# Wider loads, whole-tile stores and program order in a batched x·yᵀ kernel

## The chip, the cores and the metric

The kernel runs on one core of a Trainium2 chip. The metric is the device time of one execution in microseconds (us). A core has TensorE (PE) for matmuls, VectorE (DVE), ScalarE (ACT) and GpSimd (POOL) for elementwise work, SyncE (SP), which here issues every transfer, and 16 DMA engines that move data between device memory (HBM) and on-chip memory. One transfer is split over all 16 engines, and each of them adds one to the transfer's completion count.

A ratio is the mean time of one kernel's fast runs over that of the other's fast runs of the same rounds, with a 95% interval; it is not quite the ratio of the medians that are quoted.

## The reference

```python
batch, n_heads, seq_t, seq_s, channels = 8, 12, 512, 512, 64
def reference(x, y):                      # x, y: (8, 12, 512, 64) float32
    return np.einsum('bhtc,bhsc->bhts', x, y).astype(np.float32)
```

There are 96 heads, each a 512x64 by 64x512 product. Inputs are 25.2 MB, the output is 100.7 MB, so most of the traffic is stores.

## The kernel before

Eight heads make a group, twelve groups in all. A group's x and y are one load of 1 MB each: 128 partitions, two runs of 16 rows x 64 channels x 4 bytes = 4 KB. GpSimd casts to bf16, TensorE transposes, VectorE and ScalarE copy the transposes out, four 64-row matmuls fill one 128x1024 block of PSUM, and VectorE or ScalarE evicts it. A result tile is two heads, 2 MB, 16 KB in each partition, and goes out in one store, except for the first two and the last two tiles ("edge"), which go in two halves of 8 KB a partition. Loads are kept three groups ahead; six result buffers exist.

```python
    G = 4; Q = P // G; R = T // Q; NG = B * H // (2 * G); K = R // 2; AHEAD = 3
    xv = x...rearrange("(g a p n) -> g p a n", a=2, p=P, n=R * C)          # R * C * 4 = 4 KB
    lpool = ...tile_pool(name="lpool", bufs=AHEAD)
    opool = ...tile_pool(name="opool", bufs=6)
    def load(g):
        ...
        nc.sync.dma_start(ys.rearrange("p a r c -> p a (r c)"), yv[g])
        nc.sync.dma_start(xs.rearrange("p a r c -> p a (r c)"), xv[g])
    ...
    for g in range(NG):
        xT, yT = made.pop(g)
        steps = prepare(g + 1, made) if g + 1 < NG else iter(())   # next group's casts, transposes
        for a in range(2):
            for pair in range(2):
                ot = opool.tile([P, K, S], fp32)
                edge = (g == 0 and a == 0) or (g == NG - 1 and a == 1)
                for k in range(K // 2):
                    ...                                            # next(steps) at blocks 0, 3, 6 of two tiles
                    for two in range(2):
                        for h in range(2):
                            col = (2 * pair + h) * Q
                            nc.tensor.matmul(pm[h * 64:(h + 1) * 64, two, :],
                                xT[a * C:(a + 1) * C, 2 * k + two, col:col + Q]...,
                                yT[a * C:(a + 1) * C, (2 * pair + h) * S:(2 * pair + h + 1) * S], ...)
                    ...                                            # evict pm to ot: ACT or DVE
                    if edge and k % 2 == 1:
                        nc.sync.dma_start(ov[g, 2 * a + pair][:, i:j], otf[:, i:j])
                if not edge:
                    nc.sync.dma_start(ov[g, 2 * a + pair], otf)
```

Of the kernel before, what the change touches and what calls it, by code (L numbers as in the profile page):

```python
# [1 line left out]

# [5 lines left out]


@with_exitstack  # L10
def kernel(
    ctx: ExitStack,
    tc: tile.TileContext,
    x: bass.AP,
    y: bass.AP,
    out: bass.AP,
):





    nc = tc.nc
    B, H, T, C = x.shape
    _, _, S, _ = y.shape
    P = 128
    G = 4
    Q = P // G
    R = T // Q
    NG = B * H // (2 * G)  # L30
    K = R // 2
    AHEAD = 3
    fp32 = mybir.dt.float32
    bf16 = mybir.dt.bfloat16
    COPY = mybir.ActivationFunctionType.Copy
    assert C * 2 == P and S == T and R == 16

    xv = x.rearrange("b h t c -> (b h t c)").rearrange("(g a p n) -> g p a n", a=2, p=P, n=R * C)
    yv = y.rearrange("b h t c -> (b h t c)").rearrange("(g a p n) -> g p a n", a=2, p=P, n=R * C)
    ov = out.rearrange("b h t s -> (b h t s)").rearrange("(g a p n) -> g a p n", a=4, p=P, n=K * S)  # L40

    const = ctx.enter_context(tc.tile_pool(name="const", bufs=1))
    lpool = ctx.enter_context(tc.tile_pool(name="lpool", bufs=AHEAD))
    bpool = ctx.enter_context(tc.tile_pool(name="bpool", bufs=2))
    tpool = ctx.enter_context(tc.tile_pool(name="tpool", bufs=2))
    opool = ctx.enter_context(tc.tile_pool(name="opool", bufs=6))
    ptpool = ctx.enter_context(tc.tile_pool(name="ptpsum", bufs=2, space=bass.MemoryType.PSUM))
    pmpool = ctx.enter_context(tc.tile_pool(name="pmpsum", bufs=3, space=bass.MemoryType.PSUM))

    loaded = {}  # L50

    def load(g):
        xs = lpool.tile([P, 2, R, C], fp32)
        ys = lpool.tile([P, 2, R, C], fp32)
        nc.sync.dma_start(ys.rearrange("p a r c -> p a (r c)"), yv[g])  # L55
        nc.sync.dma_start(xs.rearrange("p a r c -> p a (r c)"), xv[g])  # L56
        loaded[g] = (xs, ys)

    for g in range(AHEAD):
        load(g)  # L60

    ident = const.tile([P, P], bf16)
    make_identity(nc, ident)

    def prepare(g, made):

        xs, ys = loaded.pop(g)
        yb = bpool.tile([P, R, 2, C], bf16)
        xb = bpool.tile([P, R, 2, C], bf16)
        for s, b in ((ys, yb), (xs, xb)):  # L70
            for half in range(2):
                rows = slice(half * K, (half + 1) * K)
                nc.gpsimd.tensor_copy(b[:, rows], s[:, :, rows].rearrange("p a r c -> p r a c"))  # L73
        if g + AHEAD < NG:
            load(g + AHEAD)
        yield
        yT = tpool.tile([P, G * Q, R], bf16)
        xT = tpool.tile([P, K, P, 2], bf16)
        for half in range(2):
            pt = ptpool.tile([P, K, P], bf16)  # L80
            for k in range(K):
                nc.tensor.transpose(  # L82
                    pt[:, k, :], yb[:, half * K + k].rearrange("p a c -> p (a c)"), ident
                )
            dst = yT[:, :, half * K:(half + 1) * K]
            src = pt.rearrange("p k n -> p n k")
            if half == 0:
                nc.vector.tensor_copy(dst, src)  # L88
            else:
                nc.scalar.activation(dst, src, COPY)  # L90
            yield
        for half in range(2):
            pt = ptpool.tile([P, K, P], bf16)
            for k in range(K):
                e, i = divmod(k, K // 2)
                nc.tensor.transpose(  # L96
                    pt[:, k, :], xb[:, e * K + half * K // 2 + i].rearrange("p a c -> p (a c)"), ident
                )
            dst = xT[:, half * K // 2:(half + 1) * K // 2]
            src = pt.rearrange("p (e i) n -> p i n e", e=2)  # L100
            if half == 0:
                nc.vector.tensor_copy(dst, src)  # L102
            else:
                nc.scalar.activation(dst, src, COPY)  # L104
            yield
        made[g] = (xT, yT.rearrange("p n k -> p (n k)"))

    made = {}
    for _ in prepare(0, made):
        pass  # L110
    for g in range(NG):
        xT, yT = made.pop(g)
        steps = prepare(g + 1, made) if g + 1 < NG else iter(())
        for a in range(2):
            for pair in range(2):
                ot = opool.tile([P, K, S], fp32)
                otf = ot.rearrange("p r s -> p (r s)")
                edge = (g == 0 and a == 0) or (g == NG - 1 and a == 1)
                for k in range(K // 2):
                    if (pair * K // 2 + k) in (0, 3, 6):  # L120
                        next(steps, None)
                    pm = pmpool.tile([P, 2, S], fp32)
                    for two in range(2):
                        for h in range(2):
                            col = (2 * pair + h) * Q
                            nc.tensor.matmul(  # L126
                                pm[h * 64:(h + 1) * 64, two, :],
                                xT[a * C:(a + 1) * C, 2 * k + two, col:col + Q].rearrange("c n e -> c (n e)"),
                                yT[a * C:(a + 1) * C, (2 * pair + h) * S:(2 * pair + h + 1) * S],
                                start=True, stop=True,  # L130
                            )
                    if k % 2 == 0:
                        nc.scalar.activation(ot[:, 2 * k:2 * k + 2, :], pm, COPY)  # L133
                    else:
                        nc.vector.tensor_copy(ot[:, 2 * k:2 * k + 2, :], pm)  # L135
                    if edge and k % 2 == 1:
                        i, j = (2 * k - 2) * S, (2 * k + 2) * S
                        nc.sync.dma_start(ov[g, 2 * a + pair][:, i:j], otf[:, i:j])
                if not edge:
                    nc.sync.dma_start(ov[g, 2 * a + pair], otf)  # L140


# [1 line left out]
_INS = ['x', 'y']  # L144
_OUTS = [((8, 12, 512, 512), 'float32')]


# [23 lines left out]
```

## Time and profile before

| what | before | how to read it |
|---|---|---|
| time, median of the first three runs | 306.65 us | the profile is of another, faster execution: 306.08 us, span from first to last instruction 304.3 us |
| bytes on the data queue | 125.83 MB | loads 25.2, stores 100.7 |
| data packets | 6144 of 4 KB, 1024 of 8 KB, 5632 of 16 KB | a packet is one contiguous run of one partition |
| median packet | 159, 309, 611 ns | for 4, 8 and 16 KB |
| busiest compute engine | PE, 69% | but the evictions behind it waited for stores to free result buffers: 81.2 us on ScalarE, 55.4 us on VectorE |
| last store's 16 completions | 296.63 to 303.21 us | the spread of one transfer's completions over the 16 DMA engines |

A transfer counts as landed when the slowest of its 16 engines is done. In the first load of this kernel the 16 completions lie within 0.5 us of each other, in the last store within 6.6 us. I call that spread the **lag**, the first completion the lead engine's, and the average of the 16 the mean engine's. The lines of the page are shown with the prediction.

### The profile page before, as it was taken

How to read it: one execution, taken by the hardware profiler on the slowest of the kernel's cores; microseconds unless marked ns; L12 is line 12 of the kernel's file. 1: busy time of each engine (PE TensorE's matmuls, PEld its weight loads, DVE VectorE, ACT ScalarE, POOL GpSimd, SP SyncE). 2: the span in 40 equal slices, each digit the busy share in tenths (PEclk: the TensorE clock that was granted, in tenths of full speed). 3: DMA queues.
4: the chain of work that ended last, by engine and by line, in shares of the span. 5: the costliest groups of instructions: out<-in, count | busy, mean ns of one | idle time of the engine just before them, and what ended most of it. 6: DMA issues, size and time to landing. Idle time of an engine off the chain costs nothing.

```text
span 304.3 us, 2968 instructions
## 1 busy us (share of the span) xinstructions
PE 208.5 (69%) x1152; PEld 104.6 (34%) x1152; DVE 144.7 (48%) x120; ACT 119.4 (39%) x121; POOL 49.3 (16%) x54
## 2 busy tenths in 40 slices
PE   0899999999959538928946844893897797671000
PEld 0444344555425114513613522541453443330000
DVE  0456666567446435616525733743565664443000
ACT  1454645364445224624515512542364552522000
POOL 3773220400500310230050050031000000000000
PEclk9999999999999855555555655555555555555555
DMA  7999999999999999999999999999999999999992
GB/s 283 411 410 418 436 429 423 419 442 405 445 419 419 430 431 421 420 437 424 426 426 435 414 429 433 413 433 429 433 433 429 431 433 429 428 428 433 423 420 89
DMA packets 14031, 126.03 MB, mean 414 GB/s; under 512 B 1216, under 2 KB 1216, under 8 KB 7360
## 3 DMA queue, kind: packets, MB, share of 16 engines
q1 hardware_dynamic: 14016, 125.83, 98.2%
q8 instruction: 9, 0.15, 0.2%
q14 instruction: 6, 0.05, 0.0%
HBM read 25.17 MB, written 100.66 MB: 413 GB/s over the span
## 4 chain that ended last, share of the span: by engine, by line
DMA 60%; PE 23%; DVE 4%; ACT 2%; issue 1%; POOL 1%; SPq 0%; ACTq 0%
DMA out_dram<-ot 48%; PE pm L126 17%; DMA xs<-in_x_dram 12%; PE pt L82 3%; PE pt L96 3%; DVE ot L135 2%; ACT ot L133 2%; DVE xT L102 1%; POOL xb L73 1%; SPq L55 0%; ACTq L133 0%; SPq L140 0%; ACT xT L104 0%; SPq L56 0%
## 5 line engine op out<-in xcount | busy, mean ns | idle before, releaser
L126 PE MATMUL pm<-yT,xT 64*64 64x512 bf16 x768 | 164.0, 610 | 56.0 <-ACT ot L133 53.9
L135 DVE COPY ot<-pm 128x1024 f32<-128x1024 f32 x96 | 117.2, 1223 | 113.3 <-PE pm L126 57.3
L133 ACT ACTIVATE ot<-pm 128x1024 f32<-128x1024 f32 x96 | 95.1, 1023 | 113.7 <-DMA out_dram<-ot 81.2
L126 PEld LDWEIGHTS <-xT 64*64 64x64 bf16 x768 | 66.1, 150 | 131.2 <-issue 122.7
L73 POOL CAST yb<-ys 128x1024 bf16<-128x1024 f32 x24 | 24.3, 1040 | 140.5 <-DMA ys<-in_y_dram 94.7
L82 PE MATMUL pt<-ident,yb 128*128 128x128 bf16 x192 | 23.7, 307 | 10.7 <-POOL yb L73 6.9
L73 POOL CAST xb<-xs 128x1024 bf16<-128x1024 f32 x24 | 24.3, 1040 | 16.3 <-issue 6.9
L82 PEld LDWEIGHTS <-yb 128*128 128x128 bf16 x192 | 19.9, 143 | 20.3 <-issue 11.5
L96 PE MATMUL pt<-ident,xb 128*128 128x128 bf16 x192 | 24.9, 310 | 1.1 <-POOL xb L73 0.9
L96 PEld LDWEIGHTS <-xb 128*128 128x128 bf16 x192 | 19.1, 141 | 19.3 <-issue 17.8
L104 ACT ACTIVATE xT<-pt 128x1024 bf16<-128x1024 bf16 x12 | 12.3, 1024 | 32.9 <-PE pt L96 29.4
L102 DVE COPY xT<-pt 128x1024 bf16<-128x1024 bf16 x12 | 14.7, 1223 | 10.8 <-PE pt L96 9.4
L88 DVE COPY yT<-pt 128x1024 bf16<-128x1024 bf16 x12 | 14.6, 1216 | 8.9 <-PE pt L82 8.9
L90 ACT ACTIVATE yT<-pt 128x1024 bf16<-128x1024 bf16 x12 | 12.3, 1022 | 9.3 <-PE pt L82 7.7
L90 ACT ACT_TABLE_LOAD x1 | 1.3, 1283 | 0.7 <-PEq L155 0.7
masks.py:199 POOL TENSOR_SCALAR_AFFINE_SELECT ident<-ident 128x128 bf16<-128x128 bf16 x1 | 0.3, 292 | 0.1
masks.py:197 POOL MEMSET ident<- 128x128 bf16 x1 | 0.2, 204 | 0.3 <-POOLq L155 0.3
L155 POOL MEMSET const-float32-0.0<- 128x1 f32 x1 | 0.1, 98 | 0.2 <-issue 0.2
L155 POOL MEMSET const-bfloat16-1.0<- 128x1 bf16 x1 | 0.1, 101 | 0.0
L155 POOL MEMSET const-uint8-127<- 128x1 uint8 x1 | 0.1, 101 | 0.0
L155 POOL MEMSET const-float32-1.0<- 128x1 f32 x1 | 0.1, 98 | 0.0
## 6 DMA issues: line engine op xcount, KB each, us to landing
out_dram<-ot SPq DMA_DIRECT2D x44, 2048.0 KB, 28.3
ys<-in_y_dram SPq DMA_DIRECT2D x12, 1024.0 KB, 20.3
xs<-in_x_dram SPq DMA_DIRECT2D x12, 1024.0 KB, 22.2
out_dram<-ot SPq DMA_DIRECT2D x8, 1024.0 KB, 21.0
```

The source lines that it names most:

```text
L73: nc.gpsimd.tensor_copy(b[:, rows], s[:, :, rows].rearrange("p a r c -> p r a c"))
L82: nc.tensor.transpose(pt[:, k, :], yb[:, half * K + k].rearrange("p a c -> p (a c)"), ident)
L88: nc.vector.tensor_copy(dst, src)
L90: nc.scalar.activation(dst, src, COPY)
L96: nc.tensor.transpose(pt[:, k, :], xb[:, e * K + half * K // 2 + i].rearrange("p a c -> p (a c)"), ident)
L102: nc.vector.tensor_copy(dst, src)
L104: nc.scalar.activation(dst, src, COPY)
L126: nc.tensor.matmul(pm[h * 64:(h + 1) * 64, two, :], xT[a * C:(a + 1) * C, 2 * k + two, col:col + Q].rearrange("c n e -> c (n e)"), yT[a * ...
L133: nc.scalar.activation(ot[:, 2 * k:2 * k + 2, :], pm, COPY)
L135: nc.vector.tensor_copy(ot[:, 2 * k:2 * k + 2, :], pm)
L155: nc = _bacc.Bacc("TRN2", target_bir_lowering=False, num_devices=1)
```

## The change

Its intent is fewer and longer runs: sixteen heads a group (six groups), two 2 MB loads for each with 8 KB runs, two groups ahead (so four load tiles of 2 MB), whole-tile stores everywhere, and every engine's instructions kept in the order in which the program states them, instead of the scheduler's order.

```diff
-    G = 4
+    G = 8                      # R = 32: runs of R * C * 4 = 8 KB
-    K = R // 2
-    AHEAD = 3
+    K = 8
+    E = R // K
+    AHEAD = 2
-    ov = ...rearrange("(g a p n) -> g a p n", a=4, p=P, n=K * S)
+    ov = ...rearrange("(o p n) -> o p n", p=P, n=K * S)
-    bpool = ctx.enter_context(tc.tile_pool(name="bpool", bufs=2))
+    xbpool = ctx.enter_context(tc.tile_pool(name="xbpool", bufs=1))
+    ybpool = ctx.enter_context(tc.tile_pool(name="ybpool", bufs=3))
+        nc.sync.dma_start(xs.rearrange("p a r c -> p a (r c)"), xv[g])
         nc.sync.dma_start(ys.rearrange("p a r c -> p a (r c)"), yv[g])
-        nc.sync.dma_start(xs.rearrange("p a r c -> p a (r c)"), xv[g])
... (prepare: x first in four casts, four transposed blocks; then y in four; the next
...  loads are issued with the last y cast)
-                    if edge and k % 2 == 1:
-                        i, j = (2 * k - 2) * S, (2 * k + 2) * S
-                        nc.sync.dma_start(ov[g, 2 * a + pair][:, i:j], otf[:, i:j])
-                if not edge:
-                    nc.sync.dma_start(ov[g, 2 * a + pair], otf)
+        nc.sync.dma_start(ov[o], ot.rearrange("p r s -> p (r s)"))
+    with tc.manual_schedule():
+        for g in range(AHEAD):
+            load(g)
...
+            for m in range(G):
+                result(g * G + m, steps)
```

More of the change, by code (lines that the diff above doesn't have):

```diff
@@ L35 @@
     COPY = mybir.ActivationFunctionType.Copy
-    assert C * 2 == P and S == T and R == 16
+    assert C * 2 == P and S == T and R == 32 and 2 * Q * E == P
     xv = x.rearrange("b h t c -> (b h t c)").rearrange("(g a p n) -> g p a n", a=2, p=P, n=R * C)
     yv = y.rearrange("b h t c -> (b h t c)").rearrange("(g a p n) -> g p a n", a=2, p=P, n=R * C)
-    ov = out.rearrange("b h t s -> (b h t s)").rearrange("(g a p n) -> g a p n", a=4, p=P, n=K * S)
+    ov = out.rearrange("b h t s -> (b h t s)").rearrange("(o p n) -> o p n", p=P, n=K * S)
     const = ctx.enter_context(tc.tile_pool(name="const", bufs=1))
     lpool = ctx.enter_context(tc.tile_pool(name="lpool", bufs=AHEAD))
-    bpool = ctx.enter_context(tc.tile_pool(name="bpool", bufs=2))
+    xbpool = ctx.enter_context(tc.tile_pool(name="xbpool", bufs=1))
+    ybpool = ctx.enter_context(tc.tile_pool(name="ybpool", bufs=3))
     tpool = ctx.enter_context(tc.tile_pool(name="tpool", bufs=2))
@@ L48 @@
     pmpool = ctx.enter_context(tc.tile_pool(name="pmpsum", bufs=3, space=bass.MemoryType.PSUM))
-    loaded = {}
+    loaded, made = {}, {}
     def load(g):
@@ L54, in load, with copy @@
         ys = lpool.tile([P, 2, R, C], fp32)
+        nc.sync.dma_start(xs.rearrange("p a r c -> p a (r c)"), xv[g])
         nc.sync.dma_start(ys.rearrange("p a r c -> p a (r c)"), yv[g])
-        nc.sync.dma_start(xs.rearrange("p a r c -> p a (r c)"), xv[g])
         loaded[g] = (xs, ys)
-    for g in range(AHEAD):
-        load(g)
-    ident = const.tile([P, P], bf16)
-    make_identity(nc, ident)
-    def prepare(g, made):
-        xs, ys = loaded.pop(g)
-        yb = bpool.tile([P, R, 2, C], bf16)
-        xb = bpool.tile([P, R, 2, C], bf16)
-        for s, b in ((ys, yb), (xs, xb)):
-            for half in range(2):
-                rows = slice(half * K, (half + 1) * K)
-                nc.gpsimd.tensor_copy(b[:, rows], s[:, :, rows].rearrange("p a r c -> p r a c"))
-        if g + AHEAD < NG:
-            load(g + AHEAD)
-        yield
-        yT = tpool.tile([P, G * Q, R], bf16)
-        xT = tpool.tile([P, K, P, 2], bf16)
-        for half in range(2):
+    def copy(j, dst, src):
+        if j % 2 == 0:
+            nc.vector.tensor_copy(dst, src)
+        else:
+            nc.scalar.activation(dst, src, COPY)
@@ new lines, in prepare @@
+    def prepare(g, ident):
+        xs, ys = loaded.pop(g)
+        xb = xbpool.tile([P, R, 2, C], bf16)
+        for j in range(E):
+            rows = slice(j * K, (j + 1) * K)
+            nc.gpsimd.tensor_copy(xb[:, rows], xs[:, :, rows].rearrange("p a r c -> p r a c"))
+        xT = tpool.tile([P, K, P, E], bf16)
+        yT = tpool.tile([P, P, R], bf16)
+        n = K // E
+        for j in range(E):
+            pt = ptpool.tile([P, K, P], bf16)
+            for e in range(E):
+                for i in range(n):
+                    nc.tensor.transpose(
+                        pt[:, e * n + i, :], xb[:, e * K + j * n + i].rearrange("p a c -> p (a c)"), ident
+                    )
+            copy(j, xT[:, j * n:(j + 1) * n], pt.rearrange("p (e i) n -> p i n e", e=E))
+            yield
+        for j in range(E):
+            rows = slice(j * K, (j + 1) * K)
+            yb = ybpool.tile([P, K, 2, C], bf16)
+            nc.gpsimd.tensor_copy(yb, ys[:, :, rows].rearrange("p a r c -> p r a c"))
+            if j == E - 1 and g + AHEAD < NG:
+                load(g + AHEAD)
@@ L80, in prepare @@
             pt = ptpool.tile([P, K, P], bf16)
             for k in range(K):
-                nc.tensor.transpose(
-                    pt[:, k, :], yb[:, half * K + k].rearrange("p a c -> p (a c)"), ident
-                )
-            dst = yT[:, :, half * K:(half + 1) * K]
-            src = pt.rearrange("p k n -> p n k")
-            if half == 0:
-                nc.vector.tensor_copy(dst, src)
-            else:
-                nc.scalar.activation(dst, src, COPY)
-            yield
-        for half in range(2):
-            pt = ptpool.tile([P, K, P], bf16)
-            for k in range(K):
-                e, i = divmod(k, K // 2)
-                nc.tensor.transpose(
-                    pt[:, k, :], xb[:, e * K + half * K // 2 + i].rearrange("p a c -> p (a c)"), ident
-                )
-            dst = xT[:, half * K // 2:(half + 1) * K // 2]
-            src = pt.rearrange("p (e i) n -> p i n e", e=2)
-            if half == 0:
-                nc.vector.tensor_copy(dst, src)
-            else:
-                nc.scalar.activation(dst, src, COPY)
-            yield
@@ L106, in prepare @@
-        made[g] = (xT, yT.rearrange("p n k -> p (n k)"))
-    made = {}
-    for _ in prepare(0, made):
-        pass
-    for g in range(NG):
-        xT, yT = made.pop(g)
-        steps = prepare(g + 1, made) if g + 1 < NG else iter(())
-        for a in range(2):
-            for pair in range(2):
-                ot = opool.tile([P, K, S], fp32)
-                otf = ot.rearrange("p r s -> p (r s)")
-                edge = (g == 0 and a == 0) or (g == NG - 1 and a == 1)
-                for k in range(K // 2):
-                    if (pair * K // 2 + k) in (0, 3, 6):
-                        next(steps, None)
-                    pm = pmpool.tile([P, 2, S], fp32)
-                    for two in range(2):
-                        for h in range(2):
-                            col = (2 * pair + h) * Q
-                            nc.tensor.matmul(
-                                pm[h * 64:(h + 1) * 64, two, :],
-                                xT[a * C:(a + 1) * C, 2 * k + two, col:col + Q].rearrange("c n e -> c (n e)"),
-                                yT[a * C:(a + 1) * C, (2 * pair + h) * S:(2 * pair + h + 1) * S],
-                                start=True, stop=True,
-                            )
-                    if k % 2 == 0:
-                        nc.scalar.activation(ot[:, 2 * k:2 * k + 2, :], pm, COPY)
-                    else:
-                        nc.vector.tensor_copy(ot[:, 2 * k:2 * k + 2, :], pm)
-                    if edge and k % 2 == 1:
-                        i, j = (2 * k - 2) * S, (2 * k + 2) * S
-                        nc.sync.dma_start(ov[g, 2 * a + pair][:, i:j], otf[:, i:j])
-                if not edge:
-                    nc.sync.dma_start(ov[g, 2 * a + pair], otf)
@@ new lines, in prepare, with result @@
+                nc.tensor.transpose(pt[:, k, :], yb[:, k].rearrange("p a c -> p (a c)"), ident)
+            copy(j, yT[:, :, rows], pt.rearrange("p k n -> p n k"))
+            yield
+        made[g] = (xT, yT.rearrange("p n r -> p (n r)"))
+    def result(o, steps):
+        g, m = divmod(o, G)
+        a, h = m // (G // 2), 2 * m % G
+        xT, yT = made[g]
+        ot = opool.tile([P, K, S], fp32)
+        for k in range(K // 2):
+            if (m * (K // 2) + k) % 3 == 1:
+                next(steps, None)
+            pm = pmpool.tile([P, 2, S], fp32)
+            for two in range(2):
+                for i in range(2):
+                    nc.tensor.matmul(
+                        pm[i * 64:(i + 1) * 64, two, :],
+                        xT[a * C:(a + 1) * C, 2 * k + two, (h + i) * Q:(h + i + 1) * Q].rearrange("c n e -> c (n e)"),
+                        yT[a * C:(a + 1) * C, (h + i) * S:(h + i + 1) * S],
+                        start=True, stop=True,
+                    )
+            copy(k + 1, ot[:, 2 * k:2 * k + 2, :], pm)
+        nc.sync.dma_start(ov[o], ot.rearrange("p r s -> p (r s)"))
@@ L144 @@
+    with tc.manual_schedule():
+        for g in range(AHEAD):
+            load(g)
+        ident = const.tile([P, P], bf16)
+        make_identity(nc, ident)
+        for _ in prepare(0, ident):
+            pass
+        for g in range(NG):
+            steps = prepare(g + 1, ident) if g + 1 < NG else iter(())
+            for m in range(G):
+                result(g * G + m, steps)
+            for _ in steps:
+                pass
 _INS = ['x', 'y']
```

## The prediction

> **What bounds the kernel now.** I read the page from the top: busy shares, then the slices, then the chain.
>
> ```profile
> span 304.3 us, 2968 instructions
> PE 208.5 (69%) x1152; PEld 104.6 (34%) x1152; DVE 144.7 (48%) x120; ACT 119.4 (39%) x121; POOL 49.3 (16%) x54
> ...
> DMA  7999999999999999999999999999999999999992
> ...
> q1 hardware_dynamic: 14016, 125.83, 98.2%
> q8 instruction: 9, 0.15, 0.2%
> ...
> HBM read 25.17 MB, written 100.66 MB: 413 GB/s over the span
> ...
> DMA 60%; PE 23%; DVE 4%; ACT 2%; issue 1%; POOL 1%; SPq 0%; ACTq 0%
> ```
>
> No compute engine is over 69% busy, while the DMA row is full in every slice but the first and the last. The data queue alone takes 98.2% of the span of 16 DMA engines. The chain that ended last is 60% DMA; the 23% of PE in it lies nearly all before 64 us, and I don't believe those pieces are the limit, because the DMA row is full while they run. So the kernel is a copy of 125.83 MB with the arithmetic hidden behind it. The bytes don't change in this diff; what can change is the cost per byte, the fill at the start, the drain at the end, and holes in between.
>
> The second view is the cost per packet. The DMA view of two stretches: only loads (6 to 22 us), only whole-tile stores (210 to 260 us).
>
> ```profile
> DMA packets 1709, 6.61 MB, mean 413 GB/s; under 512 B 96, under 2 KB 96, under 8 KB 1709
> q1 hardware_dynamic: 1709, 6.61, 102.8%
> ```
> ```profile
> DMA packets 1477, 21.51 MB, mean 430 GB/s; under 512 B 164, under 2 KB 164, under 8 KB 164
> q1 hardware_dynamic: 1476, 21.50, 100.6%
> ```
>
> The share times 16 engines times the stretch, over the data packets (the ones under 512 B are the semaphore writes, 9 ns each), gives 1.028 x 16 x 16 us / 1613 = 163 ns for a 4 KB load packet and 1.006 x 16 x 50 us / 1312 = 613 ns for a 16 KB store packet. The trace's packet records have medians of 159 ns (4 KB, x6144), 309 ns (8 KB, nearly all of them stores of today's split edge tiles) and 611 ns (16 KB). That is a line: about 9 ns a packet plus 36.8 ns per 1000 bytes, so 4 KB packets run at 412 GB/s on 16 engines, 8 KB at 424 and 16 KB at 429.
>
> The third view is the end, by stretches (columns: stretch, length, five engines' busy time and counts, PE clock, DMA share, GB/s).
>
> ```profile
> 294.00:296.00 2.00, 0.00 (x0) 0.00 (x0) 0.00 (x0) 0.00 (x0) 0.00 (x0) 0.50 1.01 426
> 296.00:298.00 2.00, 0.00 (x0) 0.00 (x0) 0.00 (x0) 0.00 (x0) 0.00 (x0) 0.50 0.69 291
> 298.00:301.00 3.00, 0.00 (x0) 0.00 (x0) 0.00 (x0) 0.00 (x0) 0.00 (x0) 0.50 0.21 87
> 301.00:304.30 3.30, 0.00 (x0) 0.00 (x0) 0.00 (x0) 0.00 (x0) 0.00 (x0) 0.50 0.06 27
> ```
>
> No engine computes after 277.6 us, so the tail is pure drain. It is uneven: 87 GB/s is some three engines' worth, 27 about one. In the landing records the last store's 16 completions run from 296.6 us to 303.2 us, a lag of 6.6 us; for the first loads the spread is 0.5 us. The lag grows in steps of up to 1.3 us, several of them at the times of the nine 16 KB instruction packets of the page's q8 line (0.9 to 1.1 us each, an engine at a time). The kernel ends when the slowest DMA engine ends.
>
> **What the Trainium skill says.** (1) "DMA: Bandwidth & Descriptors", section "Where 436 GB/s comes from", gives a fabric ceiling of 435 GB/s, and an HBM limit near 358 GB/s per core. The trace agrees with the first (430 GB/s in the store stretch) and not with the second (413 over the whole span, one core running). With 430 of 435 reached, only the loads have room. (2) The same page, "Why small descriptors are slow (HBM only)", names a fixed overhead per packet; the trace's 9 ns intercept fits that. (3) "Runtime: NRT & Kernel Launch", section "Instruction fetch mechanics": instructions are refilled in 16 KiB blocks by DMA. The trace agrees: nine such packets, and the lag steps with them. The instruction count hardly changes here, so I keep the lag.
>
> **The change part by part.**
>
> *Loads in 8 KB runs, 16 heads per load.* The 24 loads of 1 MB become 12 of 2 MB; per engine 16 packets of 4 KB become 16 of 8 KB for twice the data. Today's pure load stretch has a first completion every 2.561 us (5.29 to 23.22 us, seven loads), that is 16 x 159 ns plus the semaphore. Two of them are 5.12 us. A 2 MB load of 8 KB packets: 16 x 309 ns + 9 ns = 4.95 us. Saved: 0.17 us x 12 = 2.0 us, all on the bound. It assumes that an 8 KB read costs what an 8 KB write does; 4, 8 and 16 KB lie on one line across both directions, so I take it.
>
> *Whole-tile stores at the edges.* The four tiles stored in two halves today go as one: 2 x (8 x 309 + 9) = 4.96 us becomes 8 x 611 + 9 = 4.90 us; 0.065 x 4 = 0.3 us saved. The cost is that the first store waits for a whole tile, and the last one too. Both lie behind other transfers, as follows.
>
> *Start.* Today data flow from about 2.7 us, and the first store is issued at 16.0 us. After: x(0) lands at 2.7 + 4.95 + 0.5 = 8.2 us, four POOL casts of 1.04 us to 12.3; y(0) lands at 13.1, casts to 17.3, transposes and the last copy (0.9 + 1.0) to 19.2. The first result tile has 16 matmuls in groups of 4 at 0.99 us, and in program order it stands behind the first transposes of the next group, whose x lands at 18.1 and is cast at 22.2; so the tile is done at about 27 us (estimate). The DMA engines don't starve: four loads are queued at once and the fifth and sixth are issued at about 12 and 17 us, when POOL has freed their buffers. Six loads keep the queue full to 2.7 + 6 x 4.95 = 32.4 us, five us after the first store is ready. From there tiles come every 4.5 to 5 us (16 matmuls at 0.216 us = 3.5, plus 8 transposes at 0.115 = 0.9, plus first-round waits) against 4.85 us a tile on the queue. Tight, but covered: cost 0.
>
> *Steady state.* A group of 16 heads needs on the queue 8 x 4.85 + 2 x 4.95 = 48.7 us. PE needs 8 x 3.5 + 64 x 0.115 = 35 us, DVE 20 x 1.22 = 24 us, ACT 20 x 1.02 = 20 us, POOL 8 x 1.04 = 8 us. Program order may stall PE behind a transpose, but 14 us of slack per group and six result buffers (five tiles queued, 24 us) cover that.
>
> *Depth of two load groups instead of three.* In bytes it is 8 MB against 6. A load is issued after the fifth store of a group and wanted 11 tiles of queue time later, over 55 us; it needs 29 us of queue (median of stores today 28.3 us) and 10 of its own. Hidden.
>
> *End.* The last tile's buffer is freed when the store six before it lands, so it is made with five stores (24 us) still ahead of it: whole or half makes no difference. Lag 6.6 us and 1.1 us to the end of the span stay.
>
> Sum: 306.65 - 2.0 - 0.3 = 304.35, say 304.4 us.
>
> **Rivals.** (a) The start starves: if the first tiles came 5 to 8 us later than estimated, or SP stood on a load whose cast is late with a finished store behind it, the queue would run dry near 32 us and the kernel would be at 307 to 312. For: program order, one x cast buffer, the load of y for the next group stands ahead of the first store in SP's order. Against: five us of cover, and SP's load waits end at about 17 us. (b) PE or the evictions become the bound through in-order stalls and the lower granted clock (0.50 from 120 us on): 35 us of 48.7 would have to grow by 40%; against it, the matmul pace at 0.50 in today's trace is 32 in 6.91 us, still 0.216 each. It would be 310 or more. (c) The load gain is hidden or eaten by the slowest engine: its lag depends on which engine takes which instruction fetch, and can move by 1 to 1.5 us either way; 303 to 306. (d) The 8 KB reads are no cheaper per byte than 4 KB: 306.3.
>
> **Range and chances.** The runs of before differ by 0.2 us, so the range is mine, not theirs: lag +-1.5 us around 304.4, with rival (d) and a small starve on the upper side: 302.4 to 306.8. Faster by over 2% means under 300.5 us, which needs some 4 us more than all the overhead that I can find in packets, only possible if the lag shrinks by two thirds: 0.04. Slower by over 2% (over 312.8) needs rival (a) or (b) in full: 0.04. Within 2%: 0.92.
>
> **What would show it.** Right: load packets all 8 KB at about 309 ns and a pure load stretch at 424 GB/s in place of 413; no DMA slice under 9 tenths but the first and last; stores unchanged at 611 ns; first store at 25 to 30 us and still no hole near 32 us; tail with one or two lagging engines. Wrong: 8 KB loads at 318 ns or more; a slice with a hole between 30 and 60 us, or just after each group's loads; PE's waits on transposes in place of waits for result stores; a tail much shorter or longer than 7 us, which would mean that the lag was not the instruction fetches.

## The result, and the profile after

The changed kernel takes 306.43 us (median of four runs, 306.25 to 306.62) against 306.57 us of the kernel before in the same rounds: ratio 0.9996, interval 0.9978 to 1.0013. A second set of rounds on another chip gave 0.9999. The prediction's 304.4 us did not come: 2.3 us were to go, 0.1 us went.

The page of the changed kernel, the lines that answer to those of before:

```profile
span 304.8 us, 2949 instructions
PE 217.3 (71%) x1152; PEld 101.2 (33%) x1152; DVE 145.5 (48%) x120; ACT 119.5 (39%) x121; POOL 49.1 (16%) x54
...
DMA  7999999999999999999999999999999999999991
...
q1 hardware_dynamic: 10176, 125.83, 97.5%
q8 instruction: 9, 0.15, 0.2%
...
HBM read 25.17 MB, written 100.66 MB: 413 GB/s over the span
...
DMA 52%; PE 30%; DVE 4%; POOL 3%; ACT 2%; issue 0%; ACTq 0%; SPq 0%; POOLq 0%
```

The DMA row has no hole, so nothing starved. The packets fell from 14016 to 10176 and the queue's share from 98.2% to 97.5%, yet the rate over the span is the same 413 GB/s. The packet work is smaller and the time isn't.

The DMA view of the loads-only stretch (6 to 22 us) and of a stretch with whole-tile stores only (210 to 260 us):

```profile
DMA packets 880, 6.82 MB, mean 426 GB/s; under 512 B 48, under 2 KB 48, under 8 KB 48
q1 hardware_dynamic: 880, 6.82, 101.4%
```
```profile
DMA packets 1477, 21.54 MB, mean 431 GB/s; under 512 B 162, under 2 KB 162, under 8 KB 162
q1 hardware_dynamic: 1475, 21.51, 100.7%
```

Half as many load packets, 426 GB/s in place of 413: where loads run alone, the saving is there as predicted. Stores are unchanged. Then the drain, by stretches:

```profile
294.00:296.00 2.00, 0.00 (x0) 0.00 (x0) 0.00 (x0) 0.00 (x0) 0.00 (x0) 0.50 0.97 418
296.00:298.00 2.00, 0.00 (x0) 0.00 (x0) 0.00 (x0) 0.00 (x0) 0.00 (x0) 0.50 0.48 205
298.00:301.00 3.00, 0.00 (x0) 0.00 (x0) 0.00 (x0) 0.00 (x0) 0.00 (x0) 0.50 0.17 71
301.00:304.80 3.80, 0.00 (x0) 0.00 (x0) 0.00 (x0) 0.00 (x0) 0.00 (x0) 0.50 0.05 22
```

From 296 to 298 us the engines move 205 GB/s where the kernel before still moved 291: most engines are done earlier now. But the last stretch is as long as before: one or two engines (22 GB/s is less than one engine's worth on average) work on to the end. In the completions of the last store, two profiles of each kernel:

| last store's completions, us | before | changed |
|---|---|---|
| lead engine | 296.63, 296.70 | 296.16, 296.17 |
| mean engine | 298.69, 298.95 | 298.23, 298.07 |
| slowest engine | 303.21, 303.99 | 303.66, 304.19 |

The mean engine gained 0.7 us, not 2.3. The slowest gained nothing. (Its 0.3 us of loss is partly the choice of executions: those profiled took 306.08 and 306.85 us before, 306.54 and 307.10 us after. All runs together say -0.1 us.) So there are two questions: where the load saving went, and why the tail took the rest.

### The profile page after: what moved, and what is told of

It reads as the page before. It is cut to its first block, busy times and chain, and to the rows that moved or that the text cites. A ratio compares the mean times of both kernels' runs of the same rounds, so it can differ in the third digit from the quotient of the medians.

```text
span 304.8 us, 2949 instructions
## 1 busy us (share of the span) xinstructions
PE 217.3 (71%) x1152; PEld 101.2 (33%) x1152; DVE 145.5 (48%) x120; ACT 119.5 (39%) x121; POOL 49.1 (16%) x54
## 3 DMA queue, kind: packets, MB, share of 16 engines
q1 hardware_dynamic: 10176, 125.83, 97.5%
## 4 chain that ended last, share of the span: by engine, by line
DMA 52%; PE 30%; DVE 4%; POOL 3%; ACT 2%; issue 0%; ACTq 0%; SPq 0%; POOLq 0%
DMA out_dram<-ot 50%; PE pm L111 22%; PE pt L94 5%; PE pt L81 3%; POOL xb L73 3%; DMA xs<-in_x_dram 2%; DVE ot L63 2%; ACT ot L65 2%; DVE xT L63 1%; DVE yT L63 0%; POOL yb L89 0%; ACTq L65 0%; SPq L118 0%; POOLq L89 0%
## 5 line engine op out<-in xcount | busy, mean ns | idle before, releaser
L111 PE MATMUL pm<-yT,xT 64*64 64x512 bf16 x768 | 174.1, 627 | 46.6 <-ACT ot L65 45.0
L111 PEld LDWEIGHTS <-xT 64*64 64x64 bf16 x768 | 64.7, 157 | 128.1 <-issue 124.0
L81 PEld LDWEIGHTS <-xb 128*128 128x128 bf16 x192 | 18.4, 141 | 29.0 <-issue 16.0
L94 PEld LDWEIGHTS <-yb 128*128 128x128 bf16 x192 | 18.1, 138 | 17.6 <-issue 15.2
L65 ACT ACTIVATE xT<-pt 128x1024 bf16<-128x1024 bf16 x12 | 12.3, 1022 | 19.7 <-PE pt L81 19.7
```

The source lines that it names most:

```text
L65: nc.scalar.activation(dst, src, COPY)
L81: nc.tensor.transpose(pt[:, e * n + i, :], xb[:, e * K + j * n + i].rearrange("p a c -> p (a c)"), ident)
L94: nc.tensor.transpose(pt[:, k, :], yb[:, k].rearrange("p a c -> p (a c)"), ident)
L111: nc.tensor.matmul(pm[i * 64:(i + 1) * 64, two, :], xT[a * C:(a + 1) * C, 2 * k + two, (h + i) * Q:(h + i + 1) * Q].rearrange("c n e -> c ...
```

## The experiments

My first theory, **A**, was that the packet saving is real everywhere and that something else in the changed kernel takes it back. The rival, **B**, was that it exists only in the loads ahead of the first store. For the tail, **L** said that the lag comes from instruction traffic, **M** that it comes from reads stalled at switches between loads and stores. Every run below was also measured against the kernel before on the same chip; "ratio" is against that.

### Packet size in the changed kernel: e_4k and e_2k

```diff
-        nc.sync.dma_start(xs.rearrange("p a r c -> p a (r c)"), xv[g])   (and ys)
+        for s, v in ((xs, xv), (ys, yv)):
+            w = R * C // 2                       # // 4 in e_2k
+            for j in range(2):                   # range(4)
+                cols = slice(j * w, (j + 1) * w)
+                nc.sync.dma_start(s...[:, :, cols], v[g][:, :, cols])
```

> The changed kernel with each 2 MB load cut into two 1 MB loads by columns: packets of 4 KB again, all else the same. Theory A (the packet overhead of the pure load stretch holds everywhere, and something else in the changed kernel took the gain back): every 2 MB load costs 0.155 us more, 12 x 0.155 = 1.9 us, time 308.3 us. Theory B (loads that run between stores cost nearly the same per byte in 4 KB and 8 KB packets; only the six loads before the first store gain): at most 0.6 to 0.9 us more, time 306.4 to 307.3 us.

> The same with four pieces per load, packets of 2 KB. By the line of 9 ns per packet, a 2 KB packet is 84 ns, four of them 336 against 310 ns for one of 8 KB: 26 ns x 192 packets per engine = 5.0 us more if the overhead counts everywhere (theory A, 311.4 us). Theory B: a third to a half of that, 308 to 309 us.

Measured: e_4k 308.71 us, ratio 1.0080 (1.0068 to 1.0092); e_2k 311.82 us, ratio 1.0171. That looked like a clear win for A. It wasn't: in the trace of e_4k the first 2 MB are complete some 1.4 us later on the mean engine than in the changed kernel (9.39 us against 7.98; 0.15 us was to be expected, and over a hundred of its first packets are slow, up to 0.9 us each) and further slow packets at 60 to 64 us. A column cut reads 4 KB pieces at an 8 KB stride, which the kernel before never does. The test had changed two things.

### The same with contiguous pieces: e_4kc, and its control e_8kc (twice)

Both cut each 2 MB load into two loads that are contiguous 1 MB in HBM. e_4kc lands the two halves of each 8 KB run apart on chip, so packets are 4 KB; e_8kc does not. They were meant to differ in packet size alone. They don't quite: SyncE needs 1.29 us for the first two load instructions of e_4kc against 0.84 us in e_8kc, and the first data packet starts at 2.16 us against 1.74.

```diff
+        for s, v in ((xs, xv), (ys, yv)):
+            for a in range(2):
 e_8kc:         nc.sync.dma_start(s[:, a].rearrange("p r c -> p (r c)"), v[g][:, a])
 e_4kc:         nc.sync.dma_start(s[:, :, a].rearrange("p j r c -> p j (r c)"),
                                  v[g][:, a].rearrange("p (j m) -> p j m", j=2))
```

> The changed kernel unaltered, to have it on one chip with the next three and a second profile of its drain: 0.999 of the time before (306.0 to 306.4 us), lag of the slowest DMA engine 7 to 8 us if that is a property of the kernel, anything from 5.5 to 8.5 us if it is chance.

> The changed kernel with loads in 4 KB packets again, but each load contiguous in HBM (one 1 MB load for each half of a group's heads, the two 4 KB pieces of a run landing apart on chip), because the column-cut loads of e_4k also lost about 1 us at the very start. Theory A (the packet saving is there in full): 1.9 us over after_again. Theory B (it is there only in the first six loads): 0.6 to 0.9 us over it.

> The changed kernel with each load cut into two contiguous 1 MB loads, packets still 8 KB: the control of e_4kc, from which it differs in packet size alone. If packet size is worth what the pure load stretch says everywhere: 1.9 us under e_4kc (0.994 of before). If only in the pure stretch: 0.5 to 0.8 us under e_4kc, so 0.999 of before, with loads among stores again at about 5.0 us for 2 MB and more stalled packets (1.0 to 1.3 us on the mean engine) than e_4kc had (0.2).

> e_8kc again: 0.9974 of before if the 1 MB loads are worth 0.7 us against the changed kernel's 2 MB loads; 0.999 to 1.000 if the first result was chance.

Measured: after_again ratio 0.9999 (0.9986 to 1.0012), e_4kc 1.0013 (1.0001 to 1.0025), e_8kc 0.9974 (0.9961 to 0.9986), e_8kc2 0.9976. So 4 KB packets cost 0.4 us over the changed kernel, and 1.2 us over the control (0.0038 x 306.5, error 0.5), where A asked for 1.9 and B for 0.5 to 0.8. Some 0.4 us of it is the later start of e_4kc, which leaves 0.8. That excludes A and fits B. The traces say where it lies, with one profile of e_4kc against two of e_8kc; profiles of one kernel repeat to about 0.3 us. In mean-engine completions:

| stretch, us | e_4kc | e_8kc, e_8kc2 |
|---|---|---|
| up to the first load's completion | 5.93 | 5.37, 5.34 |
| then to the last load ahead of the first store (11 MB) | 28.22 | 27.77, 28.12 |
| then to the last store | 264.74 | 264.80, 264.56 |

From the last load ahead of the first store on, packet size is worth -0.1 to 0.2 us for half of all loads, where A asked for 0.9. Before it, 0.1 to 0.5 us; 0.08 of the first row is packets, the rest the later start. So B holds, as far as one profile of e_4kc can tell.

The stretches show the saving and a loss. First 8 KB (e_8kc): loads alone, then two stretches of the last of the three blocks of loads among stores; the last column is GB/s.

```profile
6.00:22.00 16.00, 8.49 (x68) 6.78 (x68) 4.90 (x4) 4.09 (x4) 11.62 (x12) 1.00 1.01 424
158.00:163.00 5.00, 5.00 (x32) 2.43 (x28) 2.74 (x3) 2.85 (x3) 0.00 (x0) 1.00 1.01 424
163.50:166.50 3.00, 1.57 (x8) 0.52 (x5) 0.99 (x1) 0.00 (x0) 3.00 (x4) 1.00 1.06 385
```

The same with 4 KB (e_4kc, whose stretches lie 1 us later):

```profile
6.00:22.00 16.00, 8.03 (x64) 6.61 (x65) 4.90 (x4) 3.86 (x4) 10.88 (x11) 1.00 1.03 413
159.00:164.00 5.00, 5.00 (x32) 2.68 (x32) 2.50 (x3) 2.85 (x3) 0.00 (x0) 1.00 1.02 417
164.50:167.50 3.00, 1.26 (x6) 0.34 (x3) 0.67 (x1) 0.00 (x0) 2.40 (x3) 1.00 1.07 431
```

Within a block of loads, 8 KB runs at 424 against 413 to 417, as alone. At the end of the block, where the leading engines have gone on to stores while the trailing ones still read, 8 KB falls to 385 and 4 KB holds 431. This is the worst block: at the ends of the other two e_8kc moves 421 and 421 GB/s, e_4kc 422 and 425. The DMA share is over 1 in both rows: the engines are not idle, single read packets take up to 0.7 us longer than their 309 ns. Packets that took over 60 ns more than the median sum to 1.1 to 1.2 us on the mean engine in the mixed part of e_8kc and e_8kc2, to 1.0 and 1.2 in two profiles of the changed kernel, and to 0.2 in e_4kc. That is the size of what six loads should have saved there. But it is not shown that 8 KB packets are the reason: the kernel before, with 4 KB loads and seven blocks of them among stores, has 0.7 and 1.0 us of such packets in its two profiles, and e_4k, also 4 KB, has 1.5. e_4kc, in its one profile, is the exception. What makes a read stall beside stores is not shown by any run. GpSimd casts at the same time in both rows, and in e_spread (below) stalls also came while it was idle, so I don't blame it.

### More switches between loads and stores: e_spread

```diff
+        if pending:                                    # one 1 MB load of 8 KB runs ahead
+            nc.sync.dma_start(*pending.pop(0))         # of each of four stores
         nc.sync.dma_start(ov[o], ot.rearrange("p r s -> p (r s)"))
```

> The changed kernel with each group's 4 MB of loads issued as four 1 MB loads of 8 KB packets, one ahead of each of four stores, in place of all four together. Theory S (every switch from loads to stores stalls lagging engines' reads, 0.2 to 0.5 us on the mean engine in the changed kernel's four switches): twelve more switches cost 2 to 4 us, 308.5 to 310.5 us. Rival T (a load right behind a store starts early and gains 0.12 us each time): 1 to 1.5 us less, 305 us. If both are small: 306.4 us.

Measured: 307.00 us, ratio 1.0039 (1.0019 to 1.0059). Against the changed kernel that is 1.2 us more, but the fair control is e_8kc, which has the same 1 MB loads in blocks: 2.0 us more (0.0064 x 306). Further switches from loads to stores are nine, not the twelve of the expectation: twelve single loads in place of three blocks, so 0.2 us for each. Against the changed kernel theory S missed (2 to 4 us forecast), against e_8kc it holds at its low end. T falls, and spreading loads thinly among stores is no cure.

### Program order: b_prog and a_sched

b_prog puts the kernel before under program order; a_sched takes it from the changed kernel.

```diff
 b_prog:  +    with tc.manual_schedule():        (around the body)
 a_sched: -    with tc.manual_schedule():
          +    if True:
```

> The kernel before, its instructions held to program order; nothing else changes. Theory P (program order gives back what the packets gain): 1.5 to 2 us slower than before, 308 us. Rival (order doesn't matter while the queue stays full): within 0.4 us of before.

> The changed kernel with the order left to the scheduler. Theory P: 1.5 to 2 us faster than after_again, about 304.4 us. Rival: within 0.4 us of after_again; then the loss sits in the load pattern (4 MB of reads in a row) or in the drain.

Measured: b_prog 1.0001 (0.9989 to 1.0013), a_sched 0.9987 (0.9974 to 1.0001). In the kernel before the order costs nothing, so theory P falls. In the changed kernel 0.4 us may hang on it; the intervals overlap.

### Edge stores: b_edge, b_first, b_last, and before_again

The kernel before with whole tiles at both edges, at the first, at the last; and the kernel before unaltered.

```diff
-                edge = (g == 0 and a == 0) or (g == NG - 1 and a == 1)
+                edge = False        # b_first: only g == NG - 1 and a == 1; b_last: only g == 0 and a == 0
```

> The kernel before with whole-tile 16 KB stores at both edges in place of half tiles: that part of the change alone. The prediction's term is -0.3 us (306.3 against 306.6); the profiles so far say 0.0 to -0.1, because a 1 MB store of 8 KB packets completes every 2.44 us, half of the 4.86 us of a 2 MB store. Both are inside the noise of +-0.4 us; a loss of over 0.5 us would mean that a whole tile at the edge costs something.

> The kernel before with whole-tile stores at the first edge alone (group 0), halves kept at the last. If the gain of b_edge (-1.1 us) comes from the start, 305.4 us; if from the drain, 306.5 us.

> The kernel before with whole-tile stores at the last edge alone. If the gain comes from the drain, where the slowest engine handles its last 4 MB in 32 packets and four completions per engine instead of 64... no compute runs then, so I expect little: 306.3 us; 305.4 us would put the gain there.

> The kernel before, unaltered: ratio 1.000; a second profile of its drain. If the lag of the slowest engine is a property of the kernel it is 6.3 to 6.9 us again (6.6 in both profiles in the order of before so far, 7.4 to 8.0 in five of the changed kernel's family in program order); if it is chance, anything from 5.5 to 8.5.

Measured: b_edge 305.41 us, ratio 0.9964 (0.9951 to 0.9978); b_first 0.9982; b_last 0.9990; before_again 1.0003. Whole edges alone take 1.1 us off, roughly the sum of 0.6 at the start and 0.3 at the end, and three to four times my 0.3. The mean engine doesn't show it (298.67 us against 298.69 and 298.95); the slowest does (302.84 against 303.21 and 303.99). b_edge is nearly the smallest change, and it alone beats the whole change. Two notes on the expectations: that of b_last counts wrongly (whole tiles make 16 packets and two completions per engine of the last 4 MB, half tiles 32 and four); and the lag in before_again was 7.3 us, outside the 6.3 to 6.9 that were to show a property of the kernel, so a single profile's lag is good to about 0.7 us.

### The lag: e_halfmm

```diff
-                for i in range(2):
-                    nc.tensor.matmul(pm[i * 64:(i + 1) * 64, two, :], xT[..., one head's 64 columns], yT[that head])
+                nc.tensor.matmul(pm[:, two, :], xT[..., two heads' 128 columns], yT[the first head])   # wrong on purpose
```

> The changed kernel with half of the result matmuls (128 stationary columns of two heads against one head's y: half of the output is wrong on purpose; same evictions, same transfers). TensorE's instruction stream falls from 2306 rows to 1538, nine 16 KB refills to six. Theory L (the slowest DMA engine's lag at the end, 7.5 us in the changed kernel, comes from instruction traffic): lag falls by about a third to 5 us and the time with it to 304 to 305 us. Rival M (the lag comes from read stalls at switches between loads and stores): lag and time unchanged, 306.4 us.

Measured: 304.85 us, ratio 0.9959 (0.9947 to 0.9971); half of the output is wrong. Its page, and its drain:

```profile
PE 215.6 (71%) x768; PEld 84.8 (28%) x768; DVE 145.5 (48%) x120; ACT 119.1 (39%) x121; POOL 49.0 (16%) x54
...
q8 instruction: 6, 0.10, 0.1%
```
```profile
296.00:298.00 2.00, 0.00 (x0) 0.00 (x0) 0.00 (x0) 0.00 (x0) 0.00 (x0) 1.00 0.38 164
298.00:301.00 3.00, 0.00 (x0) 0.00 (x0) 0.00 (x0) 0.00 (x0) 0.00 (x0) 1.00 0.14 60
301.00:302.60 1.60, 0.00 (x0) 0.00 (x0) 0.00 (x0) 0.00 (x0) 0.00 (x0) 1.00 0.00 0
```

TensorE is as busy as before (71%), yet 384 matmuls and their weight loads fewer end the kernel 1.2 us earlier: six refills in place of nine, no packet starts after 301 us, and the lag is 5.4 us in place of 7.5 and 8.0. L's forecast holds, M's doesn't: stalled reads sum to 1.1 us on the mean engine here, as in the changed kernel, and the lag fell all the same. But stalls are a part of the lag in both: between the two loads that complete at 111 and 116 us, with no refill near, it grows from 3.3 to 4.5 us in the changed kernel and from 3.1 to 4.3 us here. (The granted clock was 1.00 in this profile; five further runs at 0.54 took 304.54 to 305.67 us, so the clock isn't the reason.) The trace also shows a second part of the lag. In stretches of stores, one of the 16 completions falls back by some 0.1 us with every 2 MB store while the others keep pace, and some 200 of the 6144 store packets take 14 to 60 ns over their 611. In the changed kernel it stops at 274 us, about when TensorE's work ends. The slow packets go down with TensorE's instructions: 210 and 206 in the changed kernel, 144 in e_halfmm, 123 in v_bdiag below (though v_diag and v_diag2 have over 250). So TensorE's instructions are shown to matter, but not that the three refills do it: no run separates the refills from whatever else goes with an instruction. One untested rival is the writing of the profile itself, since every run has its span and clock recorded. What this traffic is, the records don't name.

### A version to beat both: v_diag, v_diag2, v_bdiag

Two heads' x side by side in 128 stationary columns, zeros in the off-diagonal blocks, so that one 128-row matmul does the work of two 64-row ones and the result is right. A tile's two heads then lie half a group apart in HBM, and columns alternate between them so that the store still names 128 partitions.

```diff
-        xT = tpool.tile([P, K, P, E], bf16)
+        xT = diag[g % 2]                                   # [P, K, P, E, 2], zeroed once at the start
-            copy(j, xT[:, j * n:(j + 1) * n], ...)
+            for a in range(2):                             # 64 partitions each, every other column
+                copy(j + a, xT[half, j * n:(j + 1) * n, :, :, a], pt[half]...)
-                for i in range(2): ... matmul of 64 rows ...
+                nc.tensor.matmul(pm[:, two, :], xT[:, 2 * k + two, m * Q:(m + 1) * Q]..., yT[:, m * S:(m + 1) * S], ...)
+    v_diag, v_diag2: opool bufs=5; v_diag2: zero fills as 32-bit words on DVE and POOL, 1 MB loads
+    v_bdiag: the same in the kernel before (eight heads, six result buffers), with edge = False
```

> A version meant to beat both: the changed kernel with half of the result matmuls and a right result. Stationary operands are block diagonal (two heads' x in 128 columns, zeros between), so one 128-row matmul makes what two 64-row ones made. TensorE's stream falls from 2306 rows to 1538, six refills in place of nine, and the drift of the slowest DMA engine with it. Theory L: as e_halfmm, 0.995 to 0.996 of before, 305.2 us, lag about 5.4 us. Rival: five result buffers in place of six, and stores that alternate between two heads' areas, cost as much: 0.999 to 1.001.

> v_diag with the zero fills done early (one tile by VectorE, one by GpSimd, as 32-bit words) and 1 MB loads. If only the start was at fault: 0.993 to 0.995 of before (304.4 to 305.1 us), lag 4 to 5.5 us, no hole in the DMA row. If five result buffers or the alternating store areas cost in themselves: 0.998 or more.

> The kernel before with whole-tile edge stores (alone worth -1.1 us) and block-diagonal stationary operands, 384 result matmuls in place of 768. First store at about 20 us, loads in flight to 28 us, so no hole. Theory L: lag 4 to 5 us in place of 6.2 to 7.3, time 303.5 to 304.3 us, 0.990 to 0.993 of before. If the alternating store areas or the serial half-copies cost in themselves: 0.996 or more.

v_diag took 314.61 us, ratio 1.0262, with a right result. Its DMA rows, and the stretch that lost the time:

```profile
DMA  7995669999999999999999999999999999999994
GB/s 288 425 425 223 252 268 403 436 364 394 429 434 434 433 425 418 431 432 430 433 434 412 422 430 432 433 432 432 426 428 430 432 434 434 424 432 432 426 430 193
```
```profile
24.00:46.00 22.00, 14.16 (x92) 9.36 (x93) 14.21 (x13) 12.14 (x11) 7.93 (x8) 1.00 0.63 254
```

This is the starved start that the prediction had as rival (a): four zero fills held VectorE until 19 us, the first store was issued at 40 us, and the queue ran dry near 28 us. In 22 us at 0.63 of the engines some 8 us are lost, and they never come back. v_diag2 mended the fills but its half-partition copies still ran one after another, first store at 33 us: ratio 1.0043, lag 4.1 us. From 28 to 50 us its engines ran at 0.85, some 3 us lost, so what five result buffers cost can't be read from it.

v_bdiag starts from the kernel before, whose first store (16.0 us) has twelve us of cover; its own came at 19.7 us. It took 304.16 us, ratio 0.9933 (0.9919 to 0.9946), with a right result:

```profile
span 302.3 us, 2191 instructions
PE 156.8 (52%) x768; PEld 71.0 (23%) x768; DVE 160.1 (53%) x133; ACT 137.5 (45%) x133; POOL 51.1 (17%) x55
...
q8 instruction: 6, 0.10, 0.1%
```
```profile
296.00:298.00 2.00, 0.00 (x0) 0.00 (x0) 0.00 (x0) 0.00 (x0) 0.00 (x0) 0.50 0.58 246
298.00:301.00 3.00, 0.00 (x0) 0.00 (x0) 0.00 (x0) 0.00 (x0) 0.00 (x0) 0.50 0.18 76
301.00:302.30 1.30, 0.00 (x0) 0.00 (x0) 0.00 (x0) 0.00 (x0) 0.00 (x0) 0.50 0.00 0
```

Slowest engine 301.51 us, lag 4.8 us; 2.1 us faster than the kernel before by the ratio, and so than the changed one, with 4 KB loads and 1538 rows for TensorE, at the slow edge of its forecast. About half of it is b_edge's 1.1 us. In the profiles its mean engine is 0.5 us earlier than that of the kernel before, its slowest 2.1: most of the time was in the tail.

## Why the prediction was wrong

**The bound** was right: the DMA row stayed full and no compute engine set the time. The first store came at 27.1 us with the queue covered to about 33, as worked out, and loads among stores were always in time. Every sign that the prediction named for being right came true, and the forecast was still wrong: its list looked at medians and holes, and the loss sat in neither. One of its signs of being wrong, "8 KB loads at 318 ns or more", shows only in the mean: among stores the 8 KB reads took 318.5 and 320.5 ns in the two profiles (312 alone), while the median stayed at 309.

**The step that failed first** is the load term: "Saved: 0.17 us x 12 = 2.0 us, all on the bound." The 0.17 us was read in the pure load stretch, and there it nearly holds (5.12 to 4.97 us for 2 MB, 413 to 426 GB/s). It was then multiplied by twelve, though six of the twelve loads run among stores. By the pair e_4kc and e_8kc those gained -0.1 to 0.2 us together on the mean engine, and the six ahead of the first store 0.1 to 0.5 us; loads and edges together gained 0.7 us from the kernel before to the changed one. Packet count was saved, and stalled read packets at the ends of the blocks of loads are as large as what is missing. That they took it back is argued, not shown: the kernel before has nearly as much of them (0.7 and 1.0 us against 1.2 and 1.0).

**The edge term** was too small: 0.3 us on paper, 1.1 us alone in the kernel before. It was computed from packet durations on an average engine, while in the one profile of b_edge the gain is on the slowest.

**The step that failed second** is "The instruction count hardly changes here, so I keep the lag." The mean engine finished 0.7 us earlier (average of two profiles), the slowest 0.3 us later. Steps between kernels measured against the kernel before, in us at 306.5, make the sum plain:

| from | to | step |
|---|---|---|
| before | whole-tile edges (b_edge) | -1.1 |
| b_edge | sixteen heads, program order, 4 KB runs (e_4kc) | +1.5 |
| e_4kc | 8 KB runs (e_8kc, both) | -1.2 |
| e_8kc | 2 MB loads (the changed kernel, both) | +0.7 |

They add to -0.1, each with an error of 0.4 to 0.5. The 0.4 us of e_4kc's later start is in both middle steps; without it they are about +1.1 and -0.8. That step up is the one that the prediction had not at all. In the profiles, start included, it is 0.2 us on the mean engine and 1.6 on the slowest. Over all profiles, the lag of the eight-head kernels with 1152 matmuls and transposes is 6.1 to 7.3 us (six profiles), that of the sixteen-head ones in program order, leaving out the column cuts, 6.7 to 8.0 (six profiles); a_sched had 6.4. Program order alone costs nothing in the kernel before. The ranges overlap; the average grew by 0.9 us, from 6.5 to 7.4. So that the lag grew is shown for the family, not for any single pair of profiles; which part of the regrouping makes it grow stays open, and so does the cause of the +0.7 us of 2 MB loads.

**Readings that were off without mattering.** Of the 70 us of PE in the chain before, 49 lie ahead of 64 us, not nearly all. The sum starts from 306.65 us, but the profile that it is read from is of an execution of 306.08 us. The 0.17 us sets a measured 2.561 us against a calculated 4.95; the measured saving is 0.155.

**The rivals.** (a), a starved start, did not happen here but was real: v_diag shows its price, 8 us. (b) did not happen. (c), the slowest engine eating the gain, is half of the answer. (d), 8 KB reads no cheaper than 4 KB, is the other half, but only among stores, and only as far as the pair e_4kc and e_8kc shows it.

## What to carry to other kernels

Where a full DMA queue is the bound, as here, the end is set by the slowest of the 16 engines: look at the spread of one store's completions before costing packets, because a gain on the average engine need not reach the last one. A cost per packet that is read where loads run alone must not be multiplied over loads that share the queue with stores. And a control that changes packet size must keep the pattern in memory: a column cut at a wider stride cost 2 us more here than contiguous pieces of the same size.

## What the Trainium skill lacked or had wrong

- "DMA: Bandwidth & Descriptors", section "Where 436 GB/s comes from", lets the HBM side bind HBM transfers near 358 GB/s per core. One core alone ran at 413 GB/s over the whole span and 431 in stretches of stores. The section's own figure of 425 GB/s for 16 MB agrees with the runs; the sentence lacks that its limit is for two cores that share the memory, which no run here tests.
- The same page, "Why small descriptors are slow (HBM only)", has a fixed cost per packet. It lacks that the saving can vanish beside stores: from the last load ahead of the first store on, 264.74 us with 4 KB loads (e_4kc, one profile), 264.80 and 264.56 us with 8 KB.
- "Runtime: NRT & Kernel Launch", section "Instruction fetch mechanics", calls the cost of a refill mostly hidden. In this kernel, bound by transfers, a refill holds a DMA engine for 0.9 to 1.1 us, and six in place of nine, with a third fewer TensorE instructions, gave 1.2 us (e_halfmm, ratio 0.9959 against 0.9999 of the changed kernel). How much of it is the refills' own is not separated.
- None of the pages that I read has this drift: while TensorE works, one of a store's 16 completions at a time falls back by some 0.1 us with each 2 MB store, and some 190 of 6144 packets of 16 KB take 14 to 34 ns longer.
- None of them has what a load of 4 KB pieces at an 8 KB stride costs: ratio 1.0080 against 1.0013 for contiguous 4 KB pieces.
